# A decoder block on one core: the mixer's state products turned, its order rewritten, eight expert products put aside

## The chip, the cores and the metric

The kernel runs on one core of a Trainium2 chip. The core has TensorE (PE, matrix products; PEld is its weight load), VectorE (DVE), ScalarE (ACT), GpSimd (POOL) and SyncE (SP, which here only issues DMAs), and sixteen DMA engines between the device's DRAM and the on-chip memory. The metric is device time in microseconds (us) for one execution; lower is better.

## The reference

One decoder block on 512 tokens of 2048 channels, all in float32. It has a mixer with two branches and a layer of retrieved experts.

```python
h = modulate(rmsnorm(x, g_mix), shift1, scale1)        # shifts and scales: silu(c) @ w_ada + b_ada
q, k, v, u, gate_logits = split(h @ w_in + b_in)       # 1024, 256, 256, 1024, 4096 columns
y_attn = sliding_window_attention(rope(q), rope(k), v, sinks) @ w_attn_branch   # window 128, 16 heads, 4 kv
y = s5_ssm_states(u)             # 64 groups of 16 channels, 64 complex states: y = Re(C x) + D u
z = gelu(y); y_ssm = (z * sigmoid(z @ w_glu + b_glu)) @ w_ssm_branch
g = sigmoid(gate_logits)         # two gates per channel
x = x + gate1 * ((g[0] * y_attn + g[1] * y_ssm) @ w_out)
h2 = modulate(rmsnorm(x, g_ffn), shift2, scale2)
# per token and head: 16 of 128*128 experts, by two top-16 lists of product keys, softmax gates
x = x + gate2 * sum_over_chosen(gelu(h2 . down[i]) * gate[i] * up[i])
out = rmsnorm(x, g_final)
```

## The kernel before

**Products.** A float32 product is three matmuls in a rounded format: every operand is split into a high part and the rest (`whi`/`wlo` of a weight, `h_hi`/`h_lo` of an activation), and high-high, high-low and low-high are added in one accumulator (L202 to L204 of `product`). A dense product makes 128 output channels for 512 tokens: 16 tiles of 128 inputs, 48 matmuls. `split_weights` loads a weight block of 512 KB on SyncE's queue (`raw`, four buffers), copies its high part on ScalarE (L186) and subtracts on VectorE or, for two groups of the head, on GpSimd (L188).

**Stages.** The head norms the input in five groups of channels while `ada` rows (the modulation) are reduced on VectorE (L141); `head_product` forms the eight blocks of u group by group (L440 to L442). Beside it GpSimd forms the SSM's discretized coefficients and, by doubling, a table `rc`, `rs` of rotations (`cmul`, L343 to L348), which is stored to `rot_d`. Then come the SSM and the attention with dense products between (`dense_work`: first k, v and q, then 32 blocks of gate logits). After that follow the attention branch, the GLU, the SSM branch, the output product, the queries and top-16 lists, the gates, and the experts.

**The SSM.** Eight slices of eight groups each. A slice has four parts: `ssm_slice` forms coefficients on GpSimd (L560 to L576), then on TensorE the transposes (L582) and a kernel for the inside of chunks of eight tokens (`km`, L591, L592, through DRAM into `iraw` and `intra`), then the chunk inputs (L624), a scan on VectorE, and last the outputs (L662 to L664): per group three products whose weights are coefficients and whose moving operand is 64 columns of states. Their result is stored by group; the GLU stage loads it and applies GELU (L763).

**The attention.** Sixteen blocks (`attend`), each with scores (L700), a softmax on VectorE, ScalarE and GpSimd (L714), transposes (L722) and value products (L727).

**The experts.** The first 384 tokens run over all experts densely. Gates from one-hot products (L1111) go out to `g_d` in blocks of 16 tokens (`stg`, on ScalarE's queue) and come back by group of eight experts' rows (`gt`). `fitted` is a down product (128 experts for 352 tokens, 48 matmuls, GELU). 21 of them are formed beside the gates: sixteen in buffers of their own and five in the buffers `a`. Then sixteen groups follow: eight operands are multiplied by their gates (L1178) and split, and 16 up products of 24 matmuls are formed (L1198 to L1200), which read all eight. The other tokens gather their experts' rows from DRAM (POOL, L1022) and work on VectorE (L1028, L1039), spread over the whole stage.

**What sets the order.** The order on each engine is set by a scheduler that runs the program against a model of times, by program order and priority; `tc.issue_after` holds an instruction behind another. So a change of program order changes each engine's instruction list, and the engines run their lists in order.

Of the kernel before, what the change touches and what calls it, by code (L numbers as in the profile page):

```python
# [8 lines left out]
F32 = mybir.dt.float32  # L9
F32R = mybir.dt.float32r  # L10
F16 = mybir.dt.float16
I32 = mybir.dt.int32
# [20 lines left out]
AHEAD = 500  # L33
ADA_BUFS = 4
# [3 lines left out]
EARLY = 2  # L38
A_BUFS = 5
# [21 lines left out]
def hybrid_block(tc, I, out, dbg=None):  # L61
# [118 lines left out]
    loads = []  # L180

    def split_weights(src, part, sub=tt):
# [5 lines left out]
        sub(l, r, h.bitcast(F32), op=OP.subtract)  # L188
# [242 lines left out]
    def head_product(c):  # L431
# [27 lines left out]
    y_d = dr.tile([1024, 8, 64], F32, name="y_d")  # L459
# [8 lines left out]

    ap_ = pool("ap", "left")
    qr = ap_.tile([128, 8, T], F32, name="qr")  # L470
    kr = ap_.tile([128, 2, T], F32, name="kr")
    vv = ap_.tile([128, TT, 256], F32, name="vv")
    rp = pool("rp", "left")
    rcos = rp.tile([128, T], F32, name="rcos")
    rsin = rp.tile([128, T], F32, name="rsin")
    posi = tmp.tile([128, T], I32, name="t0", tag="t0")
    ang = row("ev")
    nc.sync.dma_start(posi, I["positions"][None, :].to_broadcast([128, T]))
    nc.vector.tensor_copy(ang, posi)
    ts(ang, ang, freq, None, op0=OP.mult)  # L480
    reduce_angle(ang, rcos)
    sin_cos(rsin, rcos, ang)
    ts(rsin, rsin, sgn, None, op0=OP.mult)
# [22 lines left out]
    def dense():  # L506
        jobs = [(8 + i, rope, kr[:, i]) for i in range(2)]
        jobs += [(10 + i, value, vv[:, :, i * 128:(i + 1) * 128]) for i in range(2)]
        jobs += [(i, rope, qr[:, i]) for i in range(8)]
        last = None  # L510
        for m, finish, dst in jobs:
            o = projected(m)
            if last:
                last[0](*last[1:])
            last = finish, dst, o
            yield
        for i in range(32):
            o = projected(20 + i, 1)
            nc.scalar.dma_start(sg_d[i], o)
            if last:  # L520
                last[0](*last[1:])
                last = None
            yield

    dense_work = dense()


    with tc.issue_after(loads[-1]):
        for i, t_ in enumerate((rc, rs)):
            nc.sync.dma_start(rot_d[:, :, i], t_.rearrange("p (a b) c -> p a b c", a=8))  # L530
# [5 lines left out]
    with tc.issue_after(loads[-1]):  # L536
        nc.sync.dma_start(bass.AP(tensor=km_d.tensor, offset=km_d[0].offset + 128, ap=[[240, 128], [30720, 8], [1, 112]]),
                            zero[:, None, :].to_broadcast([128, 8, 112]))
# [7 lines left out]
    def ssm_slice(s):  # L546
# [21 lines left out]
        cl_r, cl_i = tl("cl_r", [128, 4, 16, 8]), tl("cl_i", [128, 4, 16, 8])  # L568
# [9 lines left out]
        for mt, name in zip(mts, ("mi_r", "mi_i")):  # L578
            dst = tl(name, [128, 4, 128])
# [20 lines left out]
        iraw, intra = tl("iraw", [128, 8, 128]), tl("intra", [128, 8, 16, 8])  # L600
# [3 lines left out]
        rot = tl("rot", [128, 2, 256])  # L604
# [6 lines left out]
        u = tl("uc", [128, 8, 64])  # L611
# [706 lines left out]
```

## Time and profile before

| | |
|---|---|
| time, median of 3 | 3734.87 us (3728.91 to 3746.68) |
| profiled execution | 3761.78 us, its span 3760.0 us |
| TensorE busy | 3551.0 us, 94% |
| VectorE, ScalarE, GpSimd busy | 2686.4, 1291.9, 906.7 us |
| granted TensorE clock over the span | 0.961 |
| DMA | 921.60 MB, mean 245 GB/s |

The page gives busy time per engine and, in 40 equal slices of 94 us, the clock and the DMA share. A busy TensorE need not be at full speed: its matmuls are pipelined and the granted clock has two levels, so the clock line and the matmuls' pitch have to be read beside it. A releaser in brackets is what ended an idle time.

| stage | from, us | to, us |
|---|---|---|
| head | 0 | 210.9 |
| SSM beside dense products | 210.9 | 557.3 |
| attention beside dense products | 557.3 | 929.1 |
| branches, GLU, output, queries, top-16, gates | 929.1 | 1786.3 |
| expert groups and the end | 1786.3 | 3760.0 |

### The profile page before, as it was taken

Reading aid. Unit: us, or ns where it says so; the run is one execution under the profiler, and the core shown is the slowest. Engines: PE = TensorE matmul, PEld = TensorE weight load, DVE = VectorE, ACT = ScalarE, POOL = GpSimd, SP = SyncE. Lnnn points to the kernel's source line nnn. Section 1 sums busy time; section 2 is a strip of 40 time slices with the busy share of each in tenths; the row PEclk is TensorE's granted clock in tenths of the full one; section 3 lists DMA queues with packets and bytes.
Section 4 is the critical chain, followed back from the end, with each engine's and each line's share of the span. In section 5 each row is a group of like instructions: output and inputs, shape, how many; then the busy total and the mean of one; then the engine's idle time right before and its main releaser. Section 6 shows DMA issues by size and latency. Waiting matters only on the chain.

```text
span 3760.0 us, 51345 instructions
## 1 busy us (share of the span) xinstructions
PE 3551.0 (94%) x20045; PEld 3227.8 (86%) x20045; DVE 2686.4 (71%) x4037; ACT 1291.9 (34%) x1788; POOL 906.7 (24%) x818
## 2 busy tenths in 40 slices
PE   7699999999999988999699999999999999999997
PEld 3477777777788888999699999999999999999997
DVE  7643545556874359989787788888888888877844
ACT  3232223333543342267232332233323323333333
POOL 7744530010000145310121222121221222222102
PEclk8888989999999999999899999999999999999998
DMA  8642445446964322266998898999999899978833
GB/s 287 210 156 79 126 135 179 171 159 251 335 215 167 119 88 69 86 218 241 322 351 303 329 340 338 334 334 340 347 334 344 328 335 346 342 274 310 321 128 112
DMA packets 274104, 921.60 MB, mean 245 GB/s; under 512 B 35394, under 2 KB 92866, under 8 KB 229956
## 3 DMA queue, kind: packets, MB, share of 16 engines
q1 hardware_dynamic: 204260, 533.91, 40.3%
q0 software_dynamic: 50048, 344.55, 24.9%
q10 hardware_dynamic: 19552, 39.85, 2.8%
q8 instruction: 157, 2.57, 0.3%
q14 instruction: 87, 0.71, 0.1%
HBM read 871.03 MB, written 47.12 MB: 244 GB/s over the span
## 4 chain that ended last, share of the span: by engine, by line
PE 76%; DVE 8%; DMA 7%; issue 2%; ACT 1%; POOL 1%; SPq 0%; DVEq 0%; ACTq 0%; POOLq 0%
PE mm L204 15%; PE mm L202 15%; PE mm L203 15%; PE aux L1200 8%; PE aux L1199 8%; PE aux L1198 8%; DMA gt<-g_d 3%; DMA raw<-in_up 2%; DVE wlo L188 1%; PE aux L1111 1%; DMA iraw<-km_d 1%; PE aux L664 1%; ACT whi L186 1%; PE aux L700 1%; PE aux L727 1%
## 5 line engine op out<-in xcount | busy, mean ns | idle before, releaser
L186 ACT CAST whi<-raw 128x1024 fp32r<-128x1024 f32 (+2 forms) x744 | 759.8, 1022 | 1687.3 <-PE mm L203 761.0
L188 DVE TENSOR_TENSOR wlo<-raw,whi 128x1024 fp32r<-128x1024 f32 (+2 forms) x696 | 851.6, 1224 | 424.9 <-ACT whi L186 400.8
L204 PE MATMUL mm<-h_hi,wlo 128*128 128x352 f32 (+1 forms) x2752 | 952.0, 346 | 10.4 <-DVE wlo L188 10.2
L202 PE MATMUL mm<-h_hi,whi 128*128 128x352 f32 (+1 forms) x2752 | 950.6, 345 | 5.7 <-ACT whi L186 5.7
L203 PE MATMUL mm<-h_lo,whi 128*128 128x352 f32 (+1 forms) x2752 | 947.7, 344 | 0.0
L1198 PE MATMUL aux<-wh,whi 128*128 128x352 f32 x2048 | 671.0, 328 | 50.0 <-ACT wh L192 26.9
L1200 PE MATMUL aux<-wh,wlo 128*128 128x352 f32 x2048 | 673.6, 330 | 25.5 <-DVE wlo L188 25.4
L1199 PE MATMUL aux<-wl,whi 128*128 128x352 f32 x2048 | 670.5, 327 | 2.3 <-DVE wl L193 2.3
L204 PEld LDWEIGHTS mm<-h_hi,wlo 128*128 128x128 f32 x2752 | 523.6, 190 | 44.0 <-DVE wlo L188 14.2
L202 PEld LDWEIGHTS mm<-h_hi,whi 128*128 128x128 f32 x2752 | 523.2, 190 | 37.7 <-ACT whi L186 6.7
L203 PEld LDWEIGHTS mm<-h_lo,whi 128*128 128x128 f32 x2752 | 524.8, 191 | 32.0 <-issue 4.4
L1198 PEld LDWEIGHTS aux<-wh,whi 128*128 128x128 f32 x2048 | 393.3, 192 | 56.8 <-ACT whi L186 29.7
L1200 PEld LDWEIGHTS aux<-wh,wlo 128*128 128x128 f32 x2048 | 392.9, 192 | 33.0 <-DVE wlo L188 32.7
L1199 PEld LDWEIGHTS aux<-wl,whi 128*128 128x128 f32 x2048 | 392.8, 192 | 3.3 <-DVE wl L193 3.3
L1028 DVE SCALAR_TENSOR_TENSOR rows<-rows,hrow 128x2048 f32<-128x2048 f32 x160 | 365.4, 2284 | 17.2 <-DMA rows<-in_down_rows,pick 16.9
L141 DVE SCALAR_TENSOR_TENSOR adaw<-adaw,cb 128x1024 f32<-128x1024 f32 x176 | 230.5, 1316 | 146.9 <-DMA adaw<-in_w_ada 146.7
L1022 POOL DMA_INDIRECT rows<-in_down_rows,pick x128 | 149.8, 1170 | 693.3 <-DVE rows L1028 390.3
L1039 DVE SCALAR_TENSOR_TENSOR yrow<-rows,fit,yrow 128x2048 f32<-128x2048 f32 x127 | 297.9, 2346 | 0.1
L1022 POOL DMA_INDIRECT rows<-in_up_rows,pick x128 | 146.0, 1140 | 560.1 <-DVE rows L1028 446.9
L1201 DVE SCALAR_TENSOR_TENSOR x<-aux,mod,x 128x352 f32<-128x352 f32 x256 | 148.4, 580 | 140.1 <-PE aux L1200 139.7
L214 POOL TENSOR_TENSOR rstd<-rstd,t 128x512 f32<-128x512 f32 (+2 forms) x42 | 52.8, 1258 | 610.9 <-ACT t L212 610.2
L188 POOL TENSOR_TENSOR wlo<-raw,whi 128x1024 fp32r<-128x1024 f32 (+1 forms) x48 | 104.7, 2188 | 101.1 <-ACT whi L186 99.8
(439 smaller groups left out, 4529.0 us busy)
## 6 DMA issues: line engine op xcount, KB each, us to landing
raw<-in_down SPq DMA_DIRECT2D x256, 512.0 KB
raw<-in_up SPq DMA_DIRECT2D x256, 512.0 KB
adaw<-in_w_ada SPq DMA_DIRECT2D x192, 512.0 KB
raw<-in_w_in SPq DMA_DIRECT2D x88, 512.0 KB
g_d<-stg ACTq DMA_DIRECT2D x22, 1024.0 KB
gt<-g_d SPq DMA_DIRECT2D x16, 1408.0 KB
raw<-in_w_out SPq DMA_DIRECT2D x32, 512.0 KB
raw<-in_w_query SPq DMA_DIRECT2D x32, 512.0 KB
```

What stands on the lines that cost most here:

```text
L141: stt(w, w, 1.0, cb[:, half], op0=OP.mult, op1=OP.mult, accum_out=part[:, half:half + 1])
L186: nc.scalar.copy(h, r)
L188: sub(l, r, h.bitcast(F32), op=OP.subtract)
L202: nc.tensor.matmul(p, h[:, k], (xh[kk] if isinstance(xh, list) else xh[:, kk]), start=first, stop=False)
L203: nc.tensor.matmul(p, h[:, k], (xl[kk] if isinstance(xl, list) else xl[:, kk]), start=False, stop=False)
L204: nc.tensor.matmul(p, l[:, k], (xh[kk] if isinstance(xh, list) else xh[:, kk]), start=False, stop=last)
L1022: nc.gpsimd.indirect_dma_start(out=r.rearrange("p k c -> p (k c)"), out_offset=None, in_=I[table], in_offset=bass.IndirectOffsetOnAxis(ap= ...
L1028: stt(r, r, 1.0, hrow, op0=OP.mult, op1=OP.mult, accum_out=f[:, n:n + 1])
L1039: stt(y, r, f[:, n:n + 1], y, op0=OP.mult, op1=OP.add)
L1198: nc.tensor.matmul(p, h[:, j], WH[j], start=(j == 0), stop=False)
L1199: nc.tensor.matmul(p, h[:, j], WL[j], start=False, stop=False)
L1200: nc.tensor.matmul(p, l[:, j], WH[j], start=False, stop=(j == GI - 1))
```

## The change

- **Head.** The rotation table is built in a function that is called after the third group's last product, and is held behind that group's last weight subtract. The stores of the table to `rot_d` move from SyncE's queue to GpSimd's, and so does a store of zeros into `km_d`.
- **SSM.** In the output products states are the weights now (64 wide) and coefficients move (128 columns), for two halves of the partitions by turns; a copy `y`, sixteen small products with the identity, and GELU follow in the slice. `y_d` holds the result of GELU, and the rows of the GLU's and the branch's weights are reordered on the host to match. Several slice buffers are doubled or given tiles of their own. The parts of three slices are interleaved, beside 16 blocks of gate logits; k, v and q come after.
- **Attention.** A block's scores are issued before the previous block's transposes, with one dense product (two in the first five blocks) between, held behind the scores. The blocks run head by head. `pt` has two buffers, not three.
- **Experts.** After the first sixteen down products eight more (number 21 to 28) are formed and stored to `a_d`; then the five that stay in the buffers. `form` loads the eight back.
- **Second token set.** Its rows are turned at high priority.

GpSimd's order around the weight subtracts of the head (`wlo`) and the rotations (`rc`, `rs`), before:

```order
L346 TENSOR_TENSOR rs<-rc,sn 128x32x32
...
L345 TENSOR_TENSOR rc<-rc,ra 128x32x32
L188 TENSOR_TENSOR wlo<-raw,whi 128x512
...
L348 TENSOR_TENSOR rs<-rs,ra 128x32x32
L348 TENSOR_TENSOR vi<-vi,pt_135 128x32
L188 TENSOR_TENSOR wlo<-raw,whi 128x512 x13
L544 MEMSET bd_1533 128x128
```

and of the change, the same place (the last rotations, the two stores and the first coefficients `mt` below the dots):

```order
L350 TENSOR_TENSOR vi<-vi,pt_135 128x32
L190 TENSOR_TENSOR wlo<-raw,whi 128x512 x16
L377 MEMSET rc 128x32
L378 MEMSET rs 128x32
L345 TENSOR_TENSOR cs<-vr 128x32
...
L387 DMA rot_d<-rc 1024x1x256
L349 TENSOR_TENSOR pt_135<-sn,cs 128x32
L350 TENSOR_TENSOR rs<-rs,ra 128x32x32
L387 DMA rot_d<-rs 1024x1x256
L522 MEMSET bd_1499 128x128
...
L542 TENSOR_TENSOR mt<-bre,lre 128x512
```

All sixteen subtracts stand ahead of the table now; before, the table stood ahead of them, but for its last steps, which lay among the first three.

TensorE's order at one slice's output products, before (`x_r`, `x_i` states, `cl_r`, `cl_i` and `intra` coefficients, `uj` inputs; dense products around):

```order
L662 MATMUL aux<-x_r,cl_r 128x64 x2
L202 MATMUL mm<-h_hi,whi 128x512
...
L663 MATMUL aux<-x_i,cl_i 128x64
L664 MATMUL aux<-uj,intra 128x64
L662 MATMUL aux<-x_r,cl_r 128x64
...
L582 MATMUL aux<-cst,mt 128x128 x8
```

and of the change (`y` into the products with the identity, L651, then the next slice's chunk inputs, L602):

```order
L641 MATMUL aux<-cl_r,x_r 64x128 x2
L206 MATMUL mm<-h_hi,wlo 128x512
...
L641 MATMUL aux<-cl_i,x_i 64x128 x2
L643 MATMUL aux<-intra,uj 64x128 x2
L641 MATMUL aux<-cl_r,x_r 64x128 x2
...
L651 MATMUL aux<-cst,y 64x64 x16
L602 MATMUL aux<-uc,mi_r 64x64 x8
L602 MATMUL aux<-uc,mi_i 64x64 x8
L560 MATMUL aux<-cst,mt 128x128 x4
```

The 24 products stand in pairs of 128 columns now and are followed, 22 dense matmuls later, by the small ones.

SyncE's queue from the end of the queries' weights on (down weights `in_down`, up weights `in_up`, gates `gt`), before:

```order
L184 DMA raw<-in_w_query 128x1024 x27
L184 DMA raw<-in_down 128x1024 x42
L184 DMA raw<-in_up 128x1024 x6
L1170 DMA gt<-g_d 128x22x128
L1172 DMA x_14740<-x_d 128x16x384
...
L184 DMA raw<-in_up 128x1024 x2
...
L184 DMA raw<-in_up 128x1024 x24
L184 DMA raw<-in_down 128x1024 x10
```

and of the change (`a_d` holds the products put aside):

```order
L186 DMA raw<-in_down 128x1024 x48
L1220 DMA gt<-g_d 128x22x128
L1222 DMA x_15373<-x_d 128x16x384
L186 DMA raw<-in_down 128x1024 x3
...
L186 DMA raw<-in_down 128x1024 x4
...
L186 DMA raw<-in_up 128x1024 x37
L1177 DMA a<-a_d 128x352 x5
L186 DMA raw<-in_up 128x1024
...
L1177 DMA a<-a_d 128x352 x3
L186 DMA raw<-in_up 128x1024 x10
L186 DMA raw<-in_down 128x1024 x10
```

58 down blocks stand ahead of the up blocks where 42 did (two to a product), three groups' up blocks follow one another, and the loads of `a` are among them.

The diff, cut to its core:

```diff
-    nc.gpsimd.memset(rc[:, :, 0:1], 1.0)
-    nc.gpsimd.memset(rs[:, :, 0:1], 0.0)
-    w = 1
-    while w < 64:
-        ub, vb = (z[:, :, None].to_broadcast([128, PAIRS, w]) for z in (ur, ui))
-        cmul(rc[:, :, w:2 * w], rs[:, :, w:2 * w], rc[:, :, 0:w], rs[:, :, 0:w], ub, vb, ra[:, :, 0:w])
-        cmul(vr, vi, ur, ui, ur, ui, t0)
-        ur, ui, vr, vi = vr, vi, ur, ui
-        w *= 2
+
+    def rotations(ur, ui, vr, vi):
+        nc.gpsimd.memset(rc[:, :, 0:1], 1.0)
+        nc.gpsimd.memset(rs[:, :, 0:1], 0.0)
+        w = 1
+        while w < 64:
+            ub, vb = (z[:, :, None].to_broadcast([128, PAIRS, w]) for z in (ur, ui))
+            cmul(rc[:, :, w:2 * w], rs[:, :, w:2 * w], rc[:, :, 0:w], rs[:, :, 0:w], ub, vb, ra[:, :, 0:w])
+            cmul(vr, vi, ur, ui, ur, ui, t0)
+            ur, ui, vr, vi = vr, vi, ur, ui
+            w *= 2
+        for i, t_ in enumerate((rc, rs)):
+            nc.gpsimd.dma_start(rot_d[:, :, i], t_.rearrange("p (a b) c -> p a b c", a=8))
...
+            if c == 2 and i == 7:
+
+                with tc.issue_after(subs[-1]):
+                    rotations(ur, ui, vr, vi)
...
-    y_d = dr.tile([1024, 8, 64], F32, name="y_d")
+    y_d = dr.tile([8, 128, T], F32, name="y_d")
...
+    dense_work = gate_logits(range(16))
...
+        ta, w_r, w_i = (tl(n_, [128, 256]) for n_ in ("ta", "w_r", "w_i"))
...
+        p = aux_tile()
+        for a in range(4):
+            for n_ in range(3):
+                for two in range(2):
+                    rows = slice(two * 64, two * 64 + 64)
+                    o = p[rows, a * 128:(a + 1) * 128]
+                    if n_ < 2:
+                        x_, cl_ = ((x_r, cl_r), (x_i, cl_i))[n_]
+                        nc.tensor.matmul(o, x_[rows, a], cl_[rows, a].rearrange("p h j -> p (h j)"), start=(n_ == 0), stop=False)
+                    else:
+                        nc.tensor.matmul(o, uj[:, 2 * a + two], intra[:, 4 * two + a].rearrange("p h j -> p (h j)"),
+                                         start=False, stop=True)
+        y = tl("y", [128, 8, 64])
+        nc.scalar.copy(y, p.rearrange("p (m j) -> p j m", j=8))
+        p = aux_tile()
+        for j in range(8):
+            for two in range(2):
+                rows = slice(two * 64, two * 64 + 64)
+                nc.tensor.matmul(p[rows, j * 64:(j + 1) * 64], y[rows, j], ident[rows, rows], start=True, stop=True)
+        zs = tl("zs", [128, T])
+        act(zs.rearrange("p (c j) -> p c j", j=8), p.rearrange("p (j c) -> p c j", j=8)[:, :, ::-1], AF.Gelu_apprx_tanh)
+        nc.scalar.dma_start(y_d[s], zs)
+
+    slices = [ssm_slice(s) for s in range(8)]
+    for s, n in ((0, 2), (1, 1)):
+        for _ in range(n):
+            next(slices[s])
+    for s in range(8):
+        next(slices[s])
+        next(dense_work)
+        if s < 7:
+            next(slices[s + 1])
+        next(slices[s], None)
+        if s < 6:
+            next(slices[s + 2])
+        next(dense_work)
+    close(ss)
...
-        y = tl("uc", [128, 8, 64])
-        for two in range(2):
-            p = aux_tile()
-            rows = slice(two * 64, two * 64 + 64)
-            for a in range(4):
-                g = 2 * a + two
-                o = p[:, a * 64:(a + 1) * 64]
-                nc.tensor.matmul(o, cl_r[rows, a].rearrange("p h j -> p (h j)"), x_r[rows, a], start=True, stop=False)
-                nc.tensor.matmul(o, cl_i[rows, a].rearrange("p h j -> p (h j)"), x_i[rows, a], start=False, stop=False)
-                nc.tensor.matmul(o, intra[:, 4 * two + a].rearrange("p h j -> p (h j)"), uj[:, g], start=False, stop=True)
-            nc.scalar.copy(y[:, two::2], p[:, 0:256].rearrange("p (a c) -> p a c", a=4))
-        nc.scalar.dma_start(chunked_ap(y_d), y)
-
-    slices = [ssm_slice(s) for s in range(8)]
-    next(slices[0])
-    for s in range(8):
-        for _ in slices[s]:
-            next(dense_work)
-        if s < 7:
-            next(slices[s + 1])
...
+    jobs = [(8, rope, kr[:, 0]), (10, value, vv[:, :, 0:128])] + [(i, rope, qr[:, i]) for i in range(4)]
+    jobs += [(9, rope, kr[:, 1]), (11, value, vv[:, :, 128:256])] + [(i, rope, qr[:, i]) for i in range(4, 8)]
...
+        gates = gate_logits(range(16, 32))
+        next(gates)
+        last[0](*last[1:])
...
-    for b in range(TT):
-        for n in range(4):
-            for _ in attend(b, n):
-                next(dense_work)
+
+    blocks = [attend(b, n) for n in range(4) for b in range(TT)]
+    next(blocks[0])
+    for i, block in enumerate(blocks):
+        with tc.issue_after(next(blocks[i + 1])) if i + 1 < len(blocks) else contextlib.nullcontext():
+            for _ in range(2 if i < 5 else 1):
+                next(dense_work, None)
+        next(block, None)
...
-        y = row("ev")
-        nc.sync.dma_start(y, y_d[k * 128:(k + 1) * 128].rearrange("p j c -> p (j c)"))
-        act(z[:, k].rearrange("p (c j) -> p c j", j=8), y.rearrange("p (j c) -> p c j", j=8)[:, :, ::-1], AF.Gelu_apprx_tanh)
+        nc.sync.dma_start(z[:, k], y_d[k])
...
-                    token_rows(hrow, *(lambda ks, z=z: z[:, ks, None, wide].bitcast(F32).to_broadcast([128, 4, XQ, NX])
-                                       for z in (h2_hi, h2_lo)), (("p k (i t) -> p k i t",), {"i": XQ}))
+                    with tc.high_priority(offset=HASTE):
+                        token_rows(hrow, *(lambda ks, z=z: z[:, ks, None, wide].bitcast(F32).to_broadcast([128, 4, XQ, NX])
+                                           for z in (h2_hi, h2_lo)), (("p k (i t) -> p k i t",), {"i": XQ}))
...
+    held = EARLY * GI + A_BUFS
+    a_d = dr.tile([ASIDE, 128, ND], F32, name="a_d")
+
+    def form_aside(i2):
+        a = fitted(i2, ea.tile([128, ND], F32, name="a", bufs=A_BUFS))
+        nc.scalar.dma_start(a_d[i2 - held], a)
+
     def form(i2):
-        if i2 < 128:
+        if held <= i2 < held + ASIDE:
+            ready[i2] = ea.tile([128, ND], F32, name="a", bufs=A_BUFS)
+            nc.sync.dma_start(ready[i2], a_d[i2 - held])
+        elif i2 < 128:
             ready[i2] = fitted(i2, first.tile([128, ND], F32, name=f"a{i2}") if i2 < EARLY * GI else
                                ea.tile([128, ND], F32, name="a", bufs=A_BUFS))
 
...
             form(i2)
         return ready.pop(i2)
 
-    for i2 in range(EARLY * GI + A_BUFS):
+    for i2 in range(EARLY * GI):
+        form(i2)
+    for i2 in range(held, held + ASIDE):
+        form_aside(i2)
+    for i2 in range(EARLY * GI, held):
         form(i2)
```

## Rows read from the trace of the kernel before

**Rows 1.** The page: busy time of the engines, and the clock over 40 slices.

```profile
PE 3551.0 (94%) x20045; PEld 3227.8 (86%) x20045; DVE 2686.4 (71%) x4037; ACT 1291.9 (34%) x1788; POOL 906.7 (24%) x818
...
PEclk8888989999999999999899999999999999999998
```

**Rows 2.** Stretches: length, busy us (instructions) of PE, PEld, DVE, ACT, POOL; clock, DMA share, GB/s.

```profile
70.00:109.70 39.70, 28.91 (x100) 20.89 (x100) 37.36 (x67) 10.89 (x19) 39.47 (x48) 0.84 0.87 307
109.70:131.00 21.30, 0.00 (x0) 0.00 (x0) 1.42 (x3) 0.00 (x0) 21.30 (x31) 0.50 0.00 0
152.00:182.00 30.00, 28.31 (x122) 22.19 (x121) 28.31 (x36) 11.41 (x20) 15.55 (x10) 1.00 0.80 280
210.90:557.30 346.40, 340.25 (x1806) 268.84 (x1806) 163.15 (x289) 91.82 (x114) 170.23 (x186) 0.87 0.39 121
557.30:929.10 371.80, 371.80 (x1607) 284.46 (x1607) 208.73 (x330) 129.99 (x271) 31.05 (x16) 0.99 0.50 182
1786.30:1813.20 26.90, 0.04 (x1) 0.05 (x1) 8.72 (x11) 3.74 (x7) 4.28 (x4) 0.60 0.92 332
1813.20:1954.90 141.70, 131.88 (x769) 127.34 (x770) 126.54 (x154) 40.99 (x53) 32.73 (x27) 0.96 0.93 338
1993.80:2064.70 70.90, 65.22 (x387) 64.17 (x385) 52.14 (x57) 18.47 (x21) 11.81 (x11) 0.93 0.82 300
2064.70:2127.30 62.60, 62.60 (x387) 62.32 (x387) 51.64 (x54) 22.55 (x31) 17.47 (x13) 1.00 0.90 330
```

**Rows 3.** Timeline of POOL, head: start us, us, engine, line, operation, out<-in, count.

```profile
74.51 1.33 POOL L343 TENSOR_TENSOR rc<-rc,vr 128x32 f32<-128x32 f32 x1
...
82.19 1.24 POOL L347 TENSOR_TENSOR pt<-vi,vr 128x32 f32<-128x32 f32 x1
...
121.19 0.25 POOL L347 TENSOR_TENSOR pt<-vi,vr 128x32 f32<-128x32 f32 x1
...
131.29 1.27 POOL L188 TENSOR_TENSOR wlo<-raw,whi 128x512 fp32r<-128x512 f32 x1
```

**Rows 4.** Timeline of PE, head, with [idle before it and its releaser].

```profile
132.61 0.80 PE L442 MATMUL aux<-h_hi,wlo 128*128 128x512 f32 x1 [28.25 <-POOL wlo L188]
```

**Rows 5.** Timeline of PE, SSM stage, one slice's short matrix products.

```profile
327.80 1.12 PE L614 MATMUL aux<-uc,perm 128*128 128x512 f32 x2
...
329.29 0.69 PE L624 MATMUL aux<-uc,mi_r 128*64 128x64 f32 x16
...
346.08 0.43 PE L664 MATMUL aux<-uj,intra 128*128 128x64 f32 x2
...
347.03 0.43 PE L664 MATMUL aux<-uj,intra 128*128 128x64 f32 x2
```

**Rows 6.** Timeline of POOL, SSM stage, two coefficient products and one transfer's issue.

```profile
214.73 1.11 POOL L565 TENSOR_TENSOR t<-bim,lim 128x512 f32<-128x512 f32 x1
215.81 2.09 POOL L564 TENSOR_TENSOR mt<-bre,lim 128x512 f32<-128x512 f32 x1
...
331.39 1.36 POOL L601 DMA_DIRECT2D iraw<-km_d  x1 [1.48 <-DMA km_d<-km]
```

**Rows 7.** Timeline, attention stage, one block's first and last step before its transposes.

```profile
634.53 1.99 PE L700 MATMUL aux<-kr,qr 64*128 64x256 f32 x8
...
645.05 1.90 POOL L714 TENSOR_TENSOR sc<-sc,sm 128x1024 f32<-128x1024 f32 x1 [19.19 <-ACT ev L489]
```

**Rows 8.** The chain that ended last, after the gates: start us, us, what.

```profile
1786.29 1.96 ACT stg L1113 x2
1788.28 11.39 DMA g_d<-stg
1799.75 11.85 DMA gt<-g_d
1812.02 3.57 DVE a L1178 x8
```

**Rows 9.** The same chain, one weight load of the expert loop.

```profile
1993.44 8.38 DMA raw<-in_up
```

More of the change, by code (lines that the diff above doesn't have):

```diff
@@ L33 @@
 AHEAD = 500
+HASTE = 2000
 ADA_BUFS = 4
@@ L38 @@
 EARLY = 2
+ASIDE = 8
 A_BUFS = 5
@@ L178, in weights @@
         return h, l
-    loads = []
+    loads, subs = [], []
     def split_weights(src, part, sub=tt):
@@ L504, in value, with gate_logits @@
         nc.scalar.copy(dst, p.rearrange("p (b c) -> p b c", b=TT))
[L506 to L517, printed above, removed]
+    def gate_logits(ids):
+        for i in ids:
             o = projected(20 + i, 1)
             nc.scalar.dma_start(sg_d[i], o)
-            if last:
-                last[0](*last[1:])
-                last = None
             yield
[L525 to L530, printed above, removed]
+    dense_work = gate_logits(range(16))
     close(st0)
@@ L535, in hybrid_block @@
     nc.gpsimd.memset(zero, 0.0)
-    with tc.issue_after(loads[-1]):
-        nc.sync.dma_start(bass.AP(tensor=km_d.tensor, offset=km_d[0].offset + 128, ap=[[240, 128], [30720, 8], [1, 112]]),
-                            zero[:, None, :].to_broadcast([128, 8, 112]))
+    nc.gpsimd.dma_start(bass.AP(tensor=km_d.tensor, offset=km_d[0].offset + 128, ap=[[240, 128], [30720, 8], [1, 112]]),
+                        zero[:, None, :].to_broadcast([128, 8, 112]))
     diag = ss.tile([32, 16], F32, name="diag")
@@ L626, in ssm_slice @@
             pv.append(p[:, 0:256])
-        ta = tl("t2", [128, 512])[:, 0:256]
-        w_r, w_i = (tl("mt", [128, 4, 16, 8], 2).rearrange("p a h j -> p (a h j)")[:, 0:256] for _ in range(2))
+        ta, w_r, w_i = (tl(n_, [128, 256]) for n_ in ("ta", "w_r", "w_i"))
         tt(w_r, pv[0], rcos_, op=OP.mult)
@@ L676, in hybrid_block @@
     close(sp)
-    close(rp)
+    ap_ = pool("ap", "left")
+    qr = ap_.tile([128, 8, T], F32, name="qr")
+    kr = ap_.tile([128, 2, T], F32, name="kr")
+    vv = ap_.tile([128, TT, 256], F32, name="vv")
+    rp = pool("rp", "left")
+    rcos = rp.tile([128, T], F32, name="rcos")
+    rsin = rp.tile([128, T], F32, name="rsin")
+    posi = tmp.tile([128, T], I32, name="t0", tag="t0")
+    ang = row("ev")
+    nc.sync.dma_start(posi, I["positions"][None, :].to_broadcast([128, T]))
+    nc.vector.tensor_copy(ang, posi)
@@ new lines, in hybrid_block, with heads @@
+    ts(ang, ang, freq, None, op0=OP.mult)
+    reduce_angle(ang, rcos)
+    sin_cos(rsin, rcos, ang)
+    ts(rsin, rsin, sgn, None, op0=OP.mult)
+    jobs = [(8, rope, kr[:, 0]), (10, value, vv[:, :, 0:128])] + [(i, rope, qr[:, i]) for i in range(4)]
+    jobs += [(9, rope, kr[:, 1]), (11, value, vv[:, :, 128:256])] + [(i, rope, qr[:, i]) for i in range(4, 8)]
+    def heads():
+        last = None
+        for m, finish_, dst in jobs:
+            o = projected(m)
+            if last:
+                last[0](*last[1:])
+            last = finish_, dst, o
+            yield
+        gates = gate_logits(range(16, 32))
+        next(gates)
+        last[0](*last[1:])
+        yield
+        yield from gates
@@ L678, in hybrid_block @@
+    dense_work = heads()
+    for _ in range(7):
+        next(dense_work)
     if "q" in dbg:
@@ L699, in attend @@
             for r in range(2):
-                nc.tensor.matmul(p[:, r, 0:wd], qr[rows, np_ * 4 + r2 * 2 + r, b * 128:(b + 1) * 128],
-                                 kr[rows, np_, k0:k0 + wd], start=True, stop=True)
+                scored = nc.tensor.matmul(p[:, r, 0:wd], qr[rows, np_ * 4 + r2 * 2 + r, b * 128:(b + 1) * 128],
+                                          kr[rows, np_, k0:k0 + wd], start=True, stop=True).ins
             stt(sv[:, 2 * r2:2 * r2 + 2], p[:, :, 0:wd], 0.125, mk[:, None, :].to_broadcast([128, 2, wd]),
```

45 lines of the change are left out of this document (17 added, 28 removed).

## The prediction

> **What bounds the kernel now.** I read the busy times and the clock line first: TensorE is busy for 94% of the span, so the span is its work, plus its waits, plus what a lower clock takes from it [rows 1]. The span is 3760.0 us and the profiled run took 3761.8, some 27 us above the median of the runs shown (3734.9). I make the sum against the profiled run and carry the difference over to the median.
>
> Next the table by stretches, to see where TensorE does not run at full speed [rows 2]. Three places stand out. From 109.7 to 131.0 it does nothing at all, at the lower clock, while the DMA share is 0.00 as well. From 210.9 to 557.3, the SSM stage, it is busy, but the mean granted clock is 0.87. From 1786.3 to 1813.2, behind the gates, it does nothing again, and from there to 1954.9 the clock is 0.96. The attention stage (557.3 to 929.1) and the down products of the expert loop (62.6 us for 387 matmuls) are full and at full clock or 0.99: an edit there pays only by its own work. A matmul of 352 columns costs 62.6 / 387 = 0.162 us, so one of 512 costs about 0.235, and a dense product of 48 about 11.3.
>
> Then the timelines say who ended each hole. In the head it is GpSimd: a weight subtract at 131.29 releases TensorE after 28.25 us [rows 3, 4]. Behind the gates it is a chain through DRAM: the last gate block is copied, stored (11.39 us), read back (11.85) and multiplied (3.57) before an up product can start [rows 8].
>
> **The head: rotations behind the subtracts.** Before, the table of rotations is built on GpSimd from 74.5 on, ahead of the subtracts that TensorE needs [rows 3]. The order shows sixteen subtracts first now, then the table. So the 28.25 us gap goes. Not all of it is gain: DMA still ran when the gap began and is idle for 21.3 us of it [rows 2], and before the gap it was at a share of 0.87, so weights limit the head anyway; the transfers made early have to be made later. I take 24, bounds 20 to 28. What is late next is the table itself. The last subtract ended near 182, now near 158; the table took 74.5 to 131.3, about 57 us, so it ends at 215; its two stores of 1 MB cost about one 11.39 us store [rows 8], 226; the first coefficients are there at about 230. TensorE starts its dense work 24 us earlier than 210.9, at 187, and does 192 matmuls (before 74) in front of the first SSM transposes: 187 + 192 x 0.235 = 232. Even, with 20 us to either side, since the table's small operations take 0.25 or 1.24 us for the same shape [rows 3].
>
> **The SSM stage.** The state products change sides. Before there are 24 matmuls of 64 columns per slice at a pitch of 0.95 / 3 = 0.317 us (three lines' worth between 346.08 and 347.03) [rows 5]: 7.6 us per slice at full clock, 61 for eight. After there are 24 of 128 columns on 64-wide weights, in pairs for the two partition halves, and 16 small products with the identity. The nearest row is the pattern of L624, eight matmuls of 64 columns on 64-wide weights in 0.69 us, 0.086 each: 24 x 0.172 + 16 x 0.086 = 5.5 us per slice, 44 in all, a gain of 17. The other end: a 512-column product takes 1.12 us, a quarter 0.28, and the small ones the old 0.317: 24 x 0.28 + 16 x 0.317 = 11.8, 94 in all, a loss of 33. I take 44, because shape and alternation are those of L624. The Trainium skill, TensorEngine Tiling (Array Packing), Key Properties, speaks against that: tiles run in parallel, but a change of tiling mode drains TensorE, and here half-row and full-row products alternate. By that rule the sum would stand near the 94; before's rows alternate too and show 0.317 whatever the cause, so they cannot tell.
>
> The clock of 0.87 means that 0.26 of 346.4 us, 90 us, ran at half speed, 1.2 of 2.4 GHz, which cost 45. The stretches of short products are what TensorE does there, and in the next stretch, where they are rarer, the clock is 0.99. After, the longest run of short products is cut to a few us with dense matmuls between. I take 35 of the 45 back; bounds 0 and 45.
>
> Against it stands that the stage is denser: 50 dense matmuls per slice instead of about 100. TensorE then has 50 x 0.235 + 5.5 + about 6 for transposes, kernel products and the rest, 23 us per slice. GpSimd has 170.2 / 8 = 21.3 us per slice [rows 2], and its block-diagonal tiles are single, so it can't begin a slice's copies before TensorE has read the last one's (about 2 us), and the read-back of the kernel waits for its store (1.5 us) [rows 6]: 24.8. Seven slices at 1.5 us more, 10 us; and two slices' set-up before TensorE has met the second, 42.6 us against some 33 us of its work, another 10. Total 20, bounds 0 and 60.
>
> **Attention.** One matmul set per block becomes denser too: 48 dense matmuls (11.3 us) cover the chain from scores to scaled weights, which took from 636.5 to 646.95, 10.4 us [rows 7], and the transposes are now followed at once by the value product, which needs ScalarE's copy in between (about 1 us). Before, some 70 dense matmuls lay there. I put 1 us on twelve blocks: 12, bounds 0 and 30. Total of the mixer: 17 + 35 - 20 - 12 = 20 gained. The order of q, k and v is the same work elsewhere; GELU moves from ScalarE behind the branch products, where TensorE runs through, to ScalarE in the stage, idle for most of it (91.8 of 346.4 us): nothing.
>
> **Eight products aside.** After the gates the order shows eight down products (387 matmuls, 62.6 us) where the chain of 1.96 + 11.39 + 11.85 + 3.57 us ran bare; it is covered twice over, so the 26.9 us go, and with them about 6 us of half clock in the next stretch (0.04 of 141.7 us, doubled, and half of it lost). The work itself is the same: 16 + 8 products are only formed earlier. A new wait comes: group 2's last three operands are read back from DRAM into buffers that its own first operands free. They are issued on SyncE when VectorE has finished those, so the first lands after about the 8.38 us of a load in the loop [rows 9], while three groups' up products stand back to back with nothing else for TensorE to do. I charge 8 (bounds 2 and 14). SyncE also holds the up weights behind these loads, which have four buffers in hand, 70.9 / 16 = 4.4 us of work each [rows 2]. Net 25, bounds 10 and 36: the loop's DMA share is 0.82 to 0.93 at 300 to 338 GB/s, and it has to move the same bytes in less.
>
> The token set's rows at high priority stand at the same place of VectorE's order and TensorE waits for nothing there: nothing.
>
> **Sum.** 24 + 20 + 25 = 69: 3761.8 to 3693, and the median 3734.9 to 3666, with a range of its own from 3640 to 3692.
>
> **Rivals.**
> First, everything pays: head 28, 62 in the SSM stage (all the clock, no GpSimd wait), attention covered, 33 in the loop, total 123: 3612. For it: no row shows TensorE waiting in either stage today. Against: GpSimd and the attention chain come within 2 us of TensorE.
>
> Second, the SSM stage becomes GpSimd's: TensorE's faster products only turn into waits, or the low clock stays. Mixer -10 instead of 20: total 39, 3696.
>
> Third, the loop gives the hole back, because DMA sets the pace there: 24 + 20 + 5 = 49, 3686. Against: its down stretches leave no gap at 0.90.
>
> Fourth, on the other side: GpSimd at its contended price. One product of the coefficients takes 1.11 us, another of the same shape 2.09 [rows 6], beside VectorE's work; VectorE's share doubles when the slice halves. Twelve of them at 2.09 instead of 1.11 make 33 us per slice, 36.6 with the waits, against 23: 13.3 x 7 = 93, and the first two set-ups (24) and a table at its slower price (some 13) come 37 later. Without GpSimd's waits the change gains 69 + 20 = 89, so the balance is 89 - 93 - 37 = 41 lost: 3776. The change stops paying at a period of about 35 us per slice, and is slower by 0.5% at 37 to 38 (19 us more). The Trainium skill, SBUF — State Buffer, section "SBUF: two separate sides", says why the two prices could be: GpSimd and a VectorE operation with two SBUF inputs hold one port pair in turn, each for a whole instruction. The rows on GpSimd agree, 0.25 against 1.24 for one shape [rows 3].
>
> **Chances.** 0.45 for the sum, 0.20 for everything pays, 0.22 for GpSimd's stage, 0.08 for the loop, 0.05 for the slow side. The range reaches from just under the first rival to past the second's own uncertainty, 3600 to 3712. About 0.5%, 19 us, is what a measurement of this kernel can tell from no change: 3716 and below is faster. The sum gives 0.43 of its 0.45, the first rival all, the second 0.16, the third 0.07; faster 0.86, same 0.10, slower 0.04.
>
> **What would show it.** Right: no TensorE gap over 5 us before 200 and none behind the gates; the clock at 0.95 or more in the SSM stage; short waits on GpSimd there; one wait of 5 to 10 us at group 2. Wrong: TensorE waiting for coefficients over 4 us in every slice; a half-speed stretch in each slice as before; the value products waiting over 2 us in each block; or waits for weights between the up products that add up to the hole.

## The result, and the profile after

The changed kernel takes 3690.1 us (3686.8 to 3695.7, four runs), the kernel before 3740.8 (3728.9 to 3756.6). The ratio is 0.9855, 95% interval 0.9833 to 0.9876: 51 us less where 69 were forecast. The profiled execution's span is 3693.9 us, 66 below the one of before. That is more than the medians show: the shown profile of before is one of its longer executions.

The page of the changed kernel, busy times and clock, beside [rows 1]:

```profile
PE 3498.0 (95%) x20301; PEld 3171.9 (86%) x20301; DVE 2709.3 (73%) x4037; ACT 1271.5 (34%) x1769; POOL 906.3 (25%) x821
...
PEclk8999999999999999999999999999999999999999
```

The same columns as in [rows 2], for the head, the SSM stage (177.6 to 477), attention with the rest of the dense work (to 892.6), the eight products behind the gates (1753 to 1836, in three pieces), three groups' up products (groups 0 to 2, to 2041), and the next group's up products (group 3, counted from 0 as in the prediction; 2080 to 2142). The recorded expectations call group 3 the third group, and below "from group 3 on" means from the start of these up products to the end:

```profile
70.00:109.70 39.70, 39.23 (x161) 31.09 (x160) 38.68 (x64) 13.93 (x24) 21.84 (x21) 0.94 0.93 336
109.70:131.00 21.30, 14.80 (x54) 11.68 (x53) 20.62 (x35) 7.09 (x11) 6.28 (x4) 0.84 0.93 341
177.60:477.00 299.40, 264.73 (x1921) 201.64 (x1922) 179.85 (x281) 86.61 (x106) 195.89 (x202) 0.94 0.54 173
477.00:892.60 415.60, 400.25 (x1744) 303.07 (x1744) 216.57 (x341) 137.44 (x279) 27.71 (x16) 1.00 0.40 142
1753.00:1774.00 21.00, 16.20 (x89) 15.32 (x88) 11.52 (x11) 7.28 (x9) 6.34 (x4) 0.93 0.89 319
1774.00:1800.00 26.00, 18.32 (x82) 17.15 (x82) 14.98 (x23) 6.96 (x13) 2.66 (x2) 0.79 1.07 373
1800.00:1836.00 36.00, 35.73 (x221) 35.44 (x220) 27.14 (x31) 10.99 (x14) 5.99 (x4) 1.00 0.85 315
1836.00:2041.00 205.00, 193.93 (x1151) 187.45 (x1150) 181.00 (x204) 59.13 (x73) 48.81 (x42) 0.98 0.93 349
2080.00:2142.00 62.00, 61.87 (x387) 61.56 (x386) 53.98 (x53) 18.10 (x19) 14.61 (x12) 1.00 0.95 362
```

The first two lines answer to the hole: from 70 to 131 DMA runs at 0.93 with 336 to 341 GB/s, where it had been at 0.87 and then at nothing. (A DMA share counts the packets that start in a stretch with their whole time, so it can pass 1.) The SSM stage is shorter and its clock is 0.94, not 1; TensorE is busy for 264.7 of 299.4 us there, where it had been for 340.3 of 346.4. The last line is new: no interruption at all in a stretch that took 69 us before.

TensorE's timeline in the head, the largest wait that came in the hole's place and the first dense product, against [rows 4]:

```profile
123.61 0.80 PE L446 MATMUL aux<-h_hi,whi 128*128 128x512 f32 x1 [6.50 <-ACT h_hi L194]
...
177.57 0.79 PE L204 MATMUL mm<-h_hi,whi 128*128 128x512 f32 x1 [2.82 <-ACT whi L188]
```

GpSimd's timeline, the table's start, its two stores, and the first SSM tile behind them, against [rows 3]:

```profile
148.52 0.15 POOL L377 MEMSET rc<- 128x32 f32 x1
...
196.45 0.89 POOL L387 DMA_DIRECT2D rot_d<-rc  x1
201.40 0.86 POOL L387 DMA_DIRECT2D rot_d<-rs  x1 [0.30 <-POOL rs L350]
209.79 0.34 POOL L522 MEMSET bd<- 128x128 f32 x2 [7.53 <-DMA rot_d<-rs]
```

The dense work starts 33.3 us earlier than at 210.9; the table takes 53 us, to 201.1, and its stores have landed at 209.8.

One slice's output products, the small ones, and the next slice's first, against [rows 5]:

```profile
380.87 0.44 PE L643 MATMUL aux<-intra,uj 128*64 128x128 f32 x4
381.24 0.43 PE L641 MATMUL aux<-cl_r,x_r 64*64 64x128 f32 x4
381.51 0.39 PE L641 MATMUL aux<-cl_i,x_i 64*64 64x128 f32 x4
381.82 0.44 PE L643 MATMUL aux<-intra,uj 128*64 128x128 f32 x4
...
389.31 1.15 PE L651 MATMUL aux<-cst,y 64*64 64x64 f32 x32
390.39 0.69 PE L602 MATMUL aux<-uc,mi_r 128*64 128x64 f32 x16
...
404.57 0.43 PE L641 MATMUL aux<-cl_r,x_r 64*64 64x128 f32 x4
405.37 0.44 PE L641 MATMUL aux<-cl_i,x_i 64*64 64x128 f32 x4
```

From one L643 to the next are six matmuls in 0.95 us, 0.158 each; before it was three in 0.95. Sixteen small ones take 1.08 us. That makes 24 x 0.158 + 1.08 = 4.9 us per slice. The two lines of before that lie between those of [rows 5], at 346.08 and 347.03:

```profile
346.44 0.43 PE L662 MATMUL aux<-x_r,cl_r 64*128 64x64 f32 x2
346.72 0.38 PE L663 MATMUL aux<-x_i,cl_i 64*128 64x64 f32 x2
```

In either kernel the steps start 0.37, 0.27 and 0.31 us apart, to 0.01. A step held one product of 64 columns before and holds a pair of products of 128 columns now.

The clock behind one slice's output products, before (the stretch at 265.7 starts among them) and after (behind the last line L643 of the slice above, at 384.1):

```profile
265.70:275.90 10.20, 10.20 (x38) 8.85 (x38) 0.00 (x0) 1.92 (x4) 5.13 (x7) 0.50 0.13 35
```

```profile
384.10:394.30 10.20, 10.20 (x100) 8.43 (x99) 5.38 (x8) 2.10 (x3) 9.94 (x10) 1.00 0.49 133
```

Before, such a stretch of 7 to 14 us at half clock starts among the output products of every one of the eight slices, in five of them with no wait of TensorE near. After, one starts there, at 351.1, where TensorE comes out of a wait of 2.7 us.

The waits of TensorE by releaser in the SSM stage of the changed kernel (sum, times, longest):

```profile
PE aux L641 <- DVE x_r L627: 10.5, 4, 6.0
PE mm L206 <- DVE wlo L190: 9.2, 5, 3.3
PE mm L204 <- ACT whi L188: 7.3, 3, 2.8
PE aux L560 <- ACT zs L653: 4.7, 2, 3.3
PE aux L569 <- POOL cl_r L551: 2.9, 1, 2.9
PE aux L560 <- POOL mt L542: 1.3, 1, 1.3
PE aux L570 <- POOL cl_i L554: 1.0, 1, 1.0
```

GpSimd has 5.2 us of these; states on VectorE and weights have 27, ScalarE's GELU 4.7. Seven times from one slice's first output product to the next's, 263.8 to 473.07:

```profile
263.80:473.07 209.27, 183.49 (x1514) 138.59 (x1513) 112.07 (x208) 61.96 (x77) 121.37 (x137) 0.96 0.49 147
```

That is 29.9 us per slice (25.0 to 35.7), with TensorE busy for 26.2 and GpSimd for 17.3. VectorE's own waits in the stage for the modulation's weights, before and after:

```profile
DVE adaw L141 <- DMA adaw<-in_w_ada: 21.1, 9, 4.1
```

```profile
DVE adaw L143 <- DMA adaw<-in_w_ada: 67.3, 13, 10.7
```

### The profile page after: what moved, and what is told of

Same layout as the page of the kernel before. It is cut to its first block, busy times and chain, and to the rows that moved or that the text cites. A ratio compares the mean times of both kernels' runs of the same rounds, so it can differ in the third digit from the quotient of the medians.

```text
span 3693.9 us, 51896 instructions
## 1 busy us (share of the span) xinstructions
PE 3498.0 (95%) x20301; PEld 3171.9 (86%) x20301; DVE 2709.3 (73%) x4037; ACT 1271.5 (34%) x1769; POOL 906.3 (25%) x821
## 4 chain that ended last, share of the span: by engine, by line
PE 68%; DVE 9%; DMA 6%; issue 2%; ACT 1%; POOL 1%; DVEq 0%; SPq 0%; ACTq 0%; POOLq 0%
PE mm L204 14%; PE mm L206 14%; PE mm L205 14%; PE aux L1250 8%; PE aux L1249 7%; PE aux L1248 7%; DMA gt<-g_d 2%; DVE wlo L190 2%; DMA raw<-in_up 2%; PE aux L1146 1%; PE aux L758 1%; DMA rows<-in_up_rows,pick_x 1%; PE aux L731 1%; ACT whi L188 1%; DVE rows L1062 1%
## 5 line engine op out<-in xcount | busy, mean ns | idle before, releaser
L1250 PE MATMUL aux<-wh,wlo 128*128 128x352 f32 x2048 | 671.7, 328 | 24.8 <-DVE wlo L190 24.6
```

Source lines behind the costliest of these rows:

```text
L1250: nc.tensor.matmul(p, l[:, j], WH[j], start=False, stop=(j == GI - 1))
```

## The experiments

The three parts were each put alone into the kernel before, and in pairs. Every verdict is the ratio to the kernel before on the same chip; "us" is that ratio's distance from 1 times 3745. A single ratio is uncertain by 6 to 15 us, so I use two more readings: a mean over the four places where a part is added, and the profile's own marks.

**The kernel before again.**

> The kernel before, unchanged, for a second profile. After's profile shows the same instructions in the same order from the third expert group's down products to the end, yet they took 1613.7 us there and 1633.3 in the profile of before. Theory A: that difference is spread between executions of before (3728.9 to 3756.6 us); this profile then takes 1612 to 1628 us for that stretch. Theory B: it is an effect of the change, and the stretch takes 1630 us or more again. The hole in the head (28 us) and the one behind the gates (27 us) are there in either.

It took 3743.8 us, its span is 3742.0. From group 3 on it needs 1620.9 us; the shown profile of before had 1633.3. That is theory A's number: some 12 us are spread between executions. But the changed kernel's 1613.7 lies below either.

**The table of rotations alone.**

```diff
+            if c == 2 and i == 7:
+                with tc.issue_after(subs[-1]):
+                    rotations(ur, ui, vr, vi)      # in the kernel before, and its two stores on GpSimd
```

> The kernel before, with only the rotation table built behind the weight subtracts. In the changed kernel the dense work starts 33 us earlier. Theory A: the gap in the head is on the path, so this alone gives 24 to 33 us. Rival: the SSM stage of before starts behind the table's stores, and 74 dense matmuls do not cover a later table, so the time comes back as a wait of TensorE before the first coefficients: gain under 12 us.

3744.6 us, ratio 1.0002 (0.9979 to 1.0025): nothing, to 9 us. The gap is gone and the dense work starts at 179.1, yet the output product ends at 1315.2 instead of 1326.7. The SSM stage of the second profile of before, and of this one:

```profile
211.70:554.60 342.90, 337.41 (x1807) 266.70 (x1807) 162.91 (x289) 91.80 (x115) 170.43 (x186) 0.88 0.40 122
```

```profile
179.10:555.00 375.90, 359.26 (x1864) 284.01 (x1864) 172.57 (x296) 95.08 (x117) 189.15 (x205) 0.86 0.38 118
```

It starts 33 us earlier and ends at the same time. It holds a few more matmuls (57, some 13 us, which the next stage then lacks), waits more (16.6 instead of 5.5 us between busy times) and has the lower clock for longer (0.14 against 0.12 of the stretch lost, 11 us). The rival's number holds: 12 us of 33 reach the end of the output product. Its reason does not: waits for coefficients are 1.4 us (`mt` 1.1, `cl_i` 0.3); the in-chunk kernel (`intra`, 6.5) and weights (10.3) ended the others.

**The eight products alone.**

```diff
+    for i2 in range(held, held + ASIDE):
+        form_aside(i2)                             # in the kernel before
```

> The kernel before, with only the eight products put aside. In the changed kernel the stretch from the gates' end to the third group's up products is 13.8 us shorter, where the forecast had 25. Theory A: the eight products are limited by their weight loads, which share the DMA with the gates' read-back, so this alone gives 10 to 18 us. Rival: the hole's whole 27 us and the half clock are gained, 25 to 33 us.

3720.7 us, ratio 0.9932 (0.9904 to 0.9961): 25 us. By the total the rival's number came; by place, theory A was nearer. From the gates' end to group 3's up products it needs 330.5 us, 8 less than the 338.3 of the second profile of before (theory A had 10 to 18), and the rest takes 1596.8 instead of 1620.9.

**The mixer alone.**

```diff
-            if c == 2 and i == 7:                  # in the changed kernel: the table built where it was
-    for i2 in range(held, held + ASIDE):           # and nothing put aside
```

> The changed kernel without the head's change and without the products put aside: the mixer's exchange (and the token rows' priority) alone. Theory A: the faster state products were turned into waits, so the mixer alone gives -5 to +8 us. Rival: it gives the 20 us of the forecast, and the head's late table hid it: 15 us or more.

3742.4 us, ratio 0.9984 (0.9969 to 1.0): 6 us (0 to 12). Theory A by the total, but the output product ends 12 us earlier than in the second profile of before, so this reading alone undersells it. Its SSM stage, without the head's effect on it:

```profile
209.50:495.10 285.60, 258.48 (x1922) 198.79 (x1920) 169.52 (x278) 86.87 (x105) 160.60 (x163) 0.96 0.53 172
```

Against the second profile of before (342.9 us, busy for 337.4) it is 57 us shorter; it has less dense work beside it, and the attention stage is longer in turn (415.9 against 371.4).

**The pairs.**

> The kernel before with the rotation table built later and the eight products put aside; the mixer as before. The table alone brought the end of the output product 11.5 us forward and nothing at the end; the eight products alone brought 25 us. Theory A: the expert stage hides an earlier start only while the bare chain behind the gates is there, so the two add up here: 33 to 40 us faster than before. Rival: the expert stage takes an earlier start back in any case, by longer waits for weights: 22 to 28 us, as with the eight products alone.

3716.1 us, ratio 0.9913 (0.9884 to 0.9942): 33 us, just under theory A's range.

> The changed kernel with the rotation table where it was before: mixer and eight products. The mixer alone gave 2.6 us (an interval from 0 to 12), with the output product's end 12 us forward. Theory A: with the eight products the mixer's 12 us show: 33 to 40 us faster than before. Rival: 24 to 30 us.

3705.6 us, ratio 0.9880 (0.9841 to 0.9919): 45 us, beyond theory A.

> The changed kernel without the eight products put aside: head and mixer. In the changed kernel the output product ends 30 to 33 us earlier than before, which this one keeps. Theory A: without the eight products the expert stage gives much of it back, as after the head or the mixer alone: 5 to 18 us faster. Rival: the parts just add up, 28 us or more.

3722.2 us, ratio 0.9933 (0.9904 to 0.9961): 25 us, between the two theories.

With the changed kernel itself (0.9855, 54 us) all eight corners are there. Each part's worth, added to nothing, to either other part, and to both:

| part | added to nothing | to one | to the other | to both | mean |
|---|---|---|---|---|---|
| table later | -1 | 7 (aside) | 19 (mixer) | 9 | 9 |
| mixer | 6 | 26 (table) | 19 (aside) | 22 | 18 |
| eight aside | 25 | 33 (table) | 39 (mixer) | 29 | 32 |

A line's entries are differences of two ratios and uncertain by 6 to 18 us each; an estimate from the ratios' intervals puts each mean at some 7 us either way. So the table's 9 is barely clear of nothing.

The marks of the profiles have less spread, and say the same of where. The end of the output product: 1326.7 to 1330.5 with neither table nor mixer (three profiles), 1315.2 and 1316.2 with the table, 1314.7 and 1315.7 with the mixer, 1292.7 to 1296.3 with both (three). So the table gives 13 alone and 21 beside the mixer, and the mixer as much. From the gates' end to group 3: 334.6 to 343.1 without the eight products (five profiles), 322.2 to 333.2 with them (seven, two of them of a version below), 10 us in the mean; and from there to the end 1627 and 1610 us, 18 in the mean.

Twelve of these 18 us sit in two places. Group 3's up products take 67.9 to 71.9 us in all five profiles without the eight products, and 61.8 to 62.6 in all seven with them; six groups later it is 68.2 to 73.9 against 63.5 to 64.5, with two exceptions (68 and 72). The rest is scattered over the other groups' up products, with either sign. The chain that ended last shows the first of them, in the second profile of before:

```profile
2109.83 19.28 DMA gt<-g_d
2129.20 0.38 issue
2129.58 1.23 DVE wlo L188
```

VectorE's timeline there:

```profile
2129.14 0.52 DVE L1178 TENSOR_TENSOR a<-a,gt 128x352 f32<-128x352 f32 x1 [8.88 <-DMA gt<-g_d]
2129.58 1.22 DVE L188 TENSOR_TENSOR wlo<-raw,whi 128x1024 fp32r<-128x1024 f32 x1
```

The gates' load takes 19.3 us; a weight subtract stands behind a multiplication that waits 8.9 us for it on VectorE, and TensorE waits 5.4 us for the subtract. In the changed kernel that stretch has no wait and the clock 1.00. That the order of the loads and of VectorE's list is what did it was read, not tried by itself.

**Value products one block later** (in the changed kernel):

```diff
             pts.append(pt)
+        yield
+        po = aux_tile()
...
+        if i:
+            next(blocks[i - 1], None)
-        next(block, None)
+        next(block)
+    next(blocks[-1], None)
```

> The changed kernel with the attention's value products moved one block later, ahead of the next block's transposes, so that a dense product lies between a block's transposes and its value products. Theory A: the twelve waits of TensorE for ScalarE's copies (15.4 us) are on the path; they go, and the end of the branch stage and the whole come 10 to 16 us earlier. Rival: the chain from scores to scaled weights, or the weights, is late next and takes the waits' place: under 5 us.

3682.3 us, ratio 0.9819 (0.9789 to 0.9849), 13 us below the changed kernel's ratio: theory A. Both ran once more on one chip.

> The changed kernel again, to stand on one chip beside the version with late value products: 50 to 55 us faster than before.

> The version with the value products one block later, again. Its profile put the branch stage's end 21 us before the changed kernel's. Theory A: that holds to the end, 12 to 20 us faster than the changed kernel. Rival: the expert stage takes some back, 3 to 9 us.

3695.0 us (0.9854, 0.9824 to 0.9883) and 3679.6 (0.9813, 0.9781 to 0.9845): 15 us less, theory A. The two intervals overlap, since both carry the spread of the kernel before; the runs themselves do not (3690 to 3697 us against 3665 to 3687). Attention with its dense work, the changed kernel, its one wait there, and the version:

```profile
473.50:889.00 415.50, 400.17 (x1745) 303.40 (x1745) 216.92 (x340) 137.06 (x279) 27.69 (x16) 1.00 0.39 141
```

```profile
PE aux L758 <- ACT pt L755: 15.3, 12, 1.8
```

```profile
476.40:874.00 397.60, 397.60 (x1745) 303.97 (x1745) 221.49 (x343) 137.56 (x281) 27.68 (x16) 1.00 0.41 149
```

The same 1745 matmuls, 17.9 us less, and TensorE busy without a break.

**Four and twelve aside** (with late value products; `ASIDE = 12` in the other):

```diff
-ASIDE = 8
+ASIDE = 4
```

> Late value products, and four products put aside in place of eight: 31 us of work at full rate behind the gates, about the length of the bare chain (29 us). Theory A: what pays is that the chain is covered, and four cover it: the stretch from the gates' end to the third group stays at 322 to 330 us, the whole within 6 us of eight. Rival: the products behind the gates also stock what the DMA must bring (gates, weights), and four leave waits before the first up product: 8 to 15 us slower than eight.

3662.8 us, ratio 0.9776 (0.9738 to 0.9814): 17 us below eight on the same chip. The intervals overlap here too, the runs hardly (3658 to 3668 us against 3665 to 3687). Neither theory had that; the stretch from the gates' end to group 3 takes 318.8 us, somewhat under theory A's 322 to 330.

> Late value products, and twelve products put aside. With eight, these ran at 83 us for 62.6 us of work, short of weights while the gates are read back. Theory A: the read-back is over after eight, so four more cost their plain 31 us and nothing changes, within 6 us. Rival: the DMA stays short, and each product more loses 2 us, 6 to 12 us slower.

3694.7 us, ratio 0.9865 (0.9825 to 0.9905), 15 us above eight: worse than the rival in the total (3690 to 3705 us).

The stretch behind the gates, 1733.6 to 1783, with four (the first up products begin at 1781.5) and, 1733.4 to 1783, with eight:

```profile
1733.60:1783.00 49.40, 38.74 (x205) 36.81 (x205) 30.72 (x43) 16.75 (x25) 8.95 (x6) 0.90 0.97 348
```

```profile
1733.40:1783.00 49.60, 38.92 (x208) 37.30 (x207) 30.27 (x41) 15.83 (x24) 8.96 (x6) 0.86 0.99 353
```

The first four products take 48 us there for 31 us of work, whichever number follows: the DMA is at 0.97 to 0.99 of its time. Behind them the price is the plain one. Eight take 81 us and twelve 111 in these profiles, so four more cost 33 and 30 us; with twelve, the stretch behind the first 50 us:

```profile
1785.50:1847.10 61.60, 61.24 (x380) 60.95 (x379) 43.61 (x42) 19.64 (x23) 11.58 (x9) 1.00 0.92 339
```

By place, then, twelve behave as theory A said. The profile with four needs 318.8 us from the gates' end to group 3 and 1603.9 from there on; the two profiles with eight 322.2 and 332.3, then 1609.3 and 1611.8; the one with twelve 326.7, then 1626.1. So the 17 us that four gain are spread over both, the 15 that twelve lose lie from group 3 on, and what in the loop makes these differences the runs leave open. Four aside with late value products is the best version run: 0.9776 of the time before, against 0.9854 for the changed kernel on the same chip.

## Why the prediction was right, and where its sizes were off

The three places were named rightly, the sign too, and the size is 51 to 54 us of 69. Of the signs that the prediction named, three came and three did not: no wait between the gates and the first up product is longer than 2.8 us, GpSimd's in the SSM stage are at most 2.9, and the value products' stay under 2; but one wait of 6.5 us stands in the head, the clock of the stage is 0.94 where 0.95 was asked (0.96 with the mixer alone), and the wait at group 2 is 1.5 us and not 5 to 10. Step by step:

- **Head: 24 forecast, 33 at its end, 13 to 21 kept.** The step that put "weights limit the head anyway" was wrong: without the gap DMA ran at 0.93 where it had run at 0.87, so the whole gap and the half clock behind it went. What the sum missed is behind it: an earlier dense stage moves the table into the SSM stage's beginning, where the older mixer gave two thirds back in waits and at the lower clock. The new mixer gives back less: its stage is 14 us longer with the later table (285.6 to 299.4). In the changed kernel the table's end (201 after 53 us, forecast 215 after 57) and the first transposes (227.6, forecast 230 to 232) came as put.
- **State products: 5.5 us per slice forecast, 4.9 measured.** The size came, partly by luck: 0.172 was L624's price doubled for twice the columns, while the rows show steps that last as long as before, 0.95 us for three, with 128 columns as with 64. What halved the price of a product is that two run as a pair in one step. The Trainium skill, TensorEngine Tiling (Array Packing), Key Properties, says that a change of tiling mode drains TensorE. The rows here agree in kind: the two steps that enter another mode start 0.31 and 0.37 us behind the one before, the step that keeps the mode 0.27. That is some 0.14 us of each 0.95, in both kernels alike; what a change costs alone no run shows. The prediction's dear end of 94 us did not come; the sum is 39.
- **Clock: 35 of 45 us back forecast, about 30 measured with the mixer alone, 23 in the changed kernel.** The second profile of before loses 41 us (0.88 of 342.9), the mixer alone 11 (0.96 of 285.6), the changed kernel 18 (0.94 of 299.4). The reading holds by place too: seven of the eight half-speed stretches at the output products are gone, and each of the six stretches that the stage has left, 3 to 10 us long, lies at a wait of TensorE of 2.3 to 6 us. That shorter runs of short products did it, and not the closer order of the slices, was not tried apart.
- **Waits in the SSM stage: 20 forecast, 22 more with the mixer alone (5.5 to 27.1), 29 more in the changed kernel (34.7).** The size came; the cause failed. GpSimd ended only 5.2 us of them, and its work per slice is 17.3 us, not 21.3. The period was not GpSimd's 24.8 either: seven slices took 25.0 to 35.7 us, 29.9 in the mean, and TensorE alone is busy for 26.2 of that, where 23 were put. States that come late from VectorE (10.5), weights (16.5), whose copies and subtracts share ScalarE and VectorE with a denser slice, and GELU (4.7) ended the rest. VectorE itself waits 67 us in the stage for the modulation's weights, 21 before; whether these loads in its list make the states and subtracts late was not tried. The fourth rival's GpSimd at its contended price did not come.
- **Attention: 12 forecast, 15.4 in twelve waits**, each for ScalarE's copy. The version with late value products gets them back, which shows that they were on the path.
- **Eight aside: 25 forecast, 28 to 32 measured, in other places.** The bare chain went, but "62.6 us of work" took 83, so that only 10 us in the mean were gained up to group 3: in the middle piece the clock is 0.79 and the DMA share 1.07, bringing weights, gates and gathered rows together. The read-back of operands cost about 1.5 us, not 8:

```profile
1977.49 0.59 PE L1248 MATMUL aux<-wh,whi 128*128 128x352 f32 x2 [1.48 <-ACT wh L194]
```

The balance is made good by the rest of the loop, 18 us in the mean, which no term had. The third rival had it the other way round.

So the mixer's term (20) lies between 13 alone and 21 beside the table at the mark behind it, 18 in the mean of four, and with the mixer alone its parts came near one by one: 22 + 30 - 22 - 15 = 15. The aside's (25) came near 32 with two errors against each other, which is luck. The head's (24) is the one that carries the difference: 9 in the mean of four, 13 to 21 at the mark. The mixer was put in whole; what its turned products, the order of its slices and that of the attention are worth singly these runs do not show.

## What to carry to other kernels

A gap that is taken out of one stage is worth what the next stage can use: follow it to the next mark at which all engines meet before booking it. When work is moved to cover a chain of transfers, ask what those transfers leave of the DMA: covered work that loads weights of its own runs at the DMA's rate until they are over (here 48 us for the first 31 us of work). More cover is not better by itself: here four products beat eight and eight beat twelve, for a reason that stays open. A product that followed its operand's copy at once cost 1.3 us in each of twelve blocks here; an independent product between them took that wait away.

## What the runs showed of the hardware

Pairs of 64-wide f32 products for the two partition halves ran at 0.158 us per product of 128 columns, half of the 0.317 us that a product of 64 columns on 128-wide weights took, with twice the columns: three steps last 0.95 us in either form, and a step takes one product or a pair. At the output products of all eight slices of the kernel before, TensorE's clock fell to its lower level for 7 to 14 us, in five of them with no wait near; in the changed kernel it stayed at the upper level at seven of eight. Executions of the kernel before spread over 36 us (3731 to 3768 us in one series), those of the changed kernel over 9 and 7 in two; which waits in the expert loop make that spread was not settled.
